# The planner that orders a mixer's engines is changed, the softmax scaling leaves the score chain, and two gates move forward

## The chip, the cores and the metric

One NeuronCore of a Trainium2 chip. The time is the device time of one execution in microseconds; a kernel's time is the median over its runs. Engines are named as in the profile: PE is TensorE (PEld its weight loads), ACT ScalarE, DVE VectorE, POOL GpSimd, SP SyncE.

## What is computed

An encoder block on 512 tokens and 16 learned meta tokens, width 1024, all in float32: a half-step SwiGLU feed-forward (hidden width 2816), a mixer, and a second half-step feed-forward. The mixer is where the change lies:

```python
u = rms_norm(h, mix_norm)
z = u @ w_in                      # 42 blocks of 128 columns
y_a = hgrn2_bidir(zq_a, zi_a, zf_f, zf_b, zg_a, lb_f, lb_b, out_norm)   # 4 heads, K = V = 128
y_b = axial_gqa(zq_b, zk_b, zv_b, q_norm, k_norm, cos, sin)             # 8 heads of 64, 2 of keys
mixed = sigmoid(zgate_a) * (y_a @ w_up_a) + sigmoid(zgate_b) * (y_b @ w_up_b)
h = h + mixed @ w_out
```

`hgrn2_bidir` is a gated linear recurrence run forward and backward over chunks of 128 tokens; `axial_gqa` is softmax attention with normalised and rotated queries and keys.

## The kernel before, in words

Activations lie transposed: 128 features on the partitions, tokens along the free axis. Each weight block (128 output columns by 1024 inputs, 512 KB) is split by ScalarE and VectorE into two fp32r parts, `whi` (a cast, L90) and `wlo` (a subtraction, L92), and so are the activations (`xh`, `xl`). A product is three matmuls for each 128 inputs: a **main triple**. A block for 512 tokens is 24 matmuls, a block for all 528 is 48 in two PSUM banks.

**Mixer, main stream.** For each of four heads the main stream computes blocks of `z`: `Z_QB` (attention queries), `Z_FB`, `Z_QA`, `Z_FF`, `Z_G`, `Z_I` (backward gate, recurrence query, forward gate, output gate, value); head 0 has `Z_KB` and `Z_VB` too. Then come seven branch-b gates (`Z_GB`, `EARLY`), and eight products with `w_up_b`, each followed by its product with the gate (L1187 on). After that everything runs in a plain order: branch a, `w_out`, the second feed-forward. `scaled` (L663) takes a block out of PSUM with VectorE.

**Side chains.** Beside it run Python generators that issue instructions step by step: `prepare` (norms and rotation of keys and queries), `scores` (L841: 32 rows of attention, each a score step of four matmuls into the one `S` tile, the row's maximum `nm` on VectorE, `nr` and the Exp on ScalarE, then the reciprocal of the sum and the scaling `pr`), `turned` (L876: five transposes of a row, `ph` and `pl`, and after four rows the product with V), `gla` (L980: each head's recurrence as seven levels; a level is ScalarE's copy `ks`, four float32 matmuls into `gs`, VectorE's products on `Z` and `tot` in `grow`, and a predicated copy into `A`) and `gla_finish` (L1069: four transposes, state products, 14 closing matmuls, an rms norm by Newton steps, four transposes).

**What sets the order.** Instructions of PE, ACT, DVE and POOL stand in the order in which the Python code issues them (manual schedule, L625 and L699), and each engine takes its own in that order. The class `Order` (L161) is a planner at build time: it keeps a model time `t` of TensorE, a time at which each other engine is free, and for every chain the model time at which its next step is ready. After each triple of the main stream `tick` (L232) lets `pump` (L225) issue every chain step that is ready at `t`. Where the main stream needs something (`need`, L235), chain steps are issued, earliest first, until it is there; `t` jumps to each step's readiness. Each engine call is charged in `account` (L174). For a matmul of a side chain:

```python
if cur is not self.main:
    self.t = max(self.t, cur.ready)              # L181
...
cur.ready, cur.eng = self.t + self.DRAIN, eng    # L188, DRAIN = 0.3
```

so each matmul of a step is taken to start no earlier than 0.3 us behind the one before it. A transpose is charged 0.11 us, an fp32r matmul n/2400 + 0.0133, a float32 one at least 4n/2400 + 0.005 (L183 to L187).

Three PSUM banks `mm` are shared by the main stream and the chains: `has_bank`, `take`, `give` (L243 to L258). `weights` (L648) hands the main stream a block's two parts, adds a small chain that makes the next block's parts (two buffers each), makes it ready 0.5 us later (L657) and issues steps until its cast has been issued (L659). Three buffers `tm` (L670) hold blocks of queries, keys and values; a fourth user waits for the first one's release.

Of the kernel before, what the change touches and what calls it, by code (L numbers as in the profile page):

```python
# [15 lines left out]
P = 128  # L16
# [144 lines left out]
class Order:  # L161
# [12 lines left out]
    def account(self, eng, op, args, kw):  # L174
        out = kw.get("out", args[0])
        n, cur = 1, self.cur
        for d in out.shape[1:]:
            n *= d
        if eng == "pe":
            if cur is not self.main:  # L180
                self.t = max(self.t, cur.ready)  # L181
            if op == "transpose":
                self.t += 0.11  # L183
            elif args[1].dtype == F32R:
                self.t += n / 2400 + 0.0133
            else:
                self.t += max(4 * n / 2400, 0.06) + 0.005  # L187
            cur.ready, cur.eng = self.t + self.DRAIN, eng  # L188
            return
        if eng == "act":  # L190
            d = n * 0.000916 + 0.115
            if "accum_out" in kw:
                d += 0.19
            f = args[2] if len(args) > 2 else kw.get("func")
            if f in (AF.Exp, AF.Sigmoid, AF.Sqrt) and f != self.table:
                self.table = f
                d += 1.28
        elif op == "reciprocal":
            d = 0.0065 * n + 0.12
        elif op == "tensor_reduce":  # L200
            d = 0.70
        elif op == "memset":
            d = 0.15
        else:
            d = (n + 160) / 960
        start = max(self.free.get(eng, 0.0), cur.ready + (self.HOP if cur.eng != eng else 0.0))
        self.free[eng] = cur.ready = start + d
        cur.eng = eng
# [4 lines left out]
    def ready(self, ch):  # L213
        return ch.ready if ch.wait is None or ch.wait() else float("inf")
# [28 lines left out]
    def has_bank(self):  # L243
        return bool(self.banks)

    def take(self):

        if self.cur is self.main:
            self.need(self.has_bank)
        r = min(self.banks)  # L250
        self.banks.remove(r)
        if self.cur is self.main:
            self.t = max(self.t, r)
        else:
            self.cur.ready = max(self.cur.ready, r)
# [24 lines left out]
def block_kernel(tc, xT, wg1, wu1, wd1, w_in, wup, wout, wg2, wu2, wd2, params,  # L280
# [18 lines left out]
    with (tc.tile_pool(name="persist", bufs=1) as sp, tc.tile_pool(name="wts", bufs=1) as wp,  # L299
# [271 lines left out]
        with tc.tile_pool(name="f1", bufs=1) as ft:  # L571
# [40 lines left out]
            order = [Z_QB, Z_KB, Z_FB, Z_VB, Z_QA, Z_FF, Z_G, Z_I]  # L612
            for hd in range(1, HEADS):
                order += [c + hd for c in (Z_QB, Z_FB, Z_QA, Z_FF, Z_G, Z_I)]
            plan = [w_in[c] for c in order]
            tiles = [w_in[Z_GB + c] for c in range(KT)] + [wup[c][:, 512:] for c in range(KT)]
            plan += tiles[:EARLY] + tiles[KT:KT + 5] + tiles[EARLY:KT] + tiles[KT + 5:]
# [7 lines left out]
        with tc.tile_pool(name="mix", bufs=1) as mp, tc.manual_schedule(engines={pe.engine}):  # L625
# [22 lines left out]
            def weights():  # L648
# [5 lines left out]
                if not W.ready:  # L654
# [4 lines left out]
                    il.need(lambda: not W.ahead_raw)  # L659
# [38 lines left out]
            with (tc.tile_pool(name="heads", bufs=1) as hp, tc.tile_pool(name="small", bufs=1) as mn,  # L698
# [139 lines left out]
                waiting = []  # L838
                out_of = [0]

                def scores():  # L841

                    for j in range(HEADS):
# [3 lines left out]
                        for e in range(2):  # L847
                            for c in range(4):
# [17 lines left out]
                                yield  # L866
                                dve.reciprocal(sm, sm)
                                yield
                                act.activation(pr, pr, AF.Copy, scale=sm)
                                waiting.append((j, e, c, pr, il.cur.ready))  # L870
# [5 lines left out]
                def turned():  # L876

                    for j in range(HEADS):
                        yb.append(mp.tile([P, SEQ], F32, name="yb", tag="yb", bufs=4))
                        for e in range(2):  # L880
# [3 lines left out]
                            for c in range(4):  # L884
                                yield lambda: waiting
                                _, _, _, pr, ready = waiting.pop(0)
# [18 lines left out]
                            yield lambda: il.banks and out_of[0] < 3  # L905
# [46 lines left out]
                def gla_inputs(hd):  # L952
# [6 lines left out]
                    yield  # L959
                    if hd:  # L960
# [3 lines left out]
                    yield  # L964
                    scaled(Z[:, 0], zcols(T))
# [23 lines left out]
                def gla_head(hd, Z, tot, q, v):  # L989
# [3 lines left out]
                    ks = kbuf()  # L993
                    dve.tensor_tensor(ks, Z[:, 0, :SEQ], Z[:, 3, :SEQ], ALU.add)
                    first = il.cur.ready
# [143 lines left out]

                for gen in (prepare(), scores(), turned(), gla(), gla_finish()):  # L1140
                    il.add(gen)
                queries(0)
                gi = gla_inputs(0)
                kz, ksq = tmp("keys"), tmp("keys")
# [8 lines left out]
                for hd in range(1, HEADS):  # L1153
                    if hd > 1:
                        il.need(lambda: f"att{hd - 2}" in il.done)
# [3 lines left out]

                def gate(sg):  # L1160
                    (o, _), = zcols(SEQ)
                    dve.tensor_tensor(sg, o, R[:, :SEQ], ALU.mult)
                    give()
# [7 lines left out]
                sgs = []  # L1171
                for c in range(EARLY):
                    sg = mp.tile([P, SEQ], F32, name="mixb", tag="mb", bufs=4) if c < 4 else tmp(f"b{c}")[:, :SEQ]
                    gate(sg)
                    sgs.append(sg)
# [3 lines left out]
                ybl = hp.tile([P, 4, SEQ], F32R, name="ybl", tag="pl")  # L1179
                for j, y in enumerate(yb):  # L1180
                    split((ybh[:, j, :], ybl[:, j, :]), y, slice(0, SEQ))
                    YB.append((ybh[:, j, :], ybl[:, j, :]))
                for sg in sgs:
                    act.activation(sg, sg, AF.Sigmoid)

                mixb = []
                for c in range(KT):  # L1187
                    if c == 5:
                        sgs.append(tmp()[:, :SEQ])
                        gate(sgs[-1])  # L1190
                        act.activation(sgs[-1], sgs[-1], AF.Sigmoid)
                    b = branch(YB)
                    m = sgs[c] if c < 4 else mp.tile([P, SEQ], F32, name="mixb", tag="yb", bufs=4)
# [115 lines left out]
```

## Time and profile before

| | us |
|---|---|
| median of 3 runs | 1239.66 (1239.02 to 1242.03) |
| the profiled execution | 1241.96 |
| its span, first to last instruction | 1240.1 |
| mean granted TensorE clock | 0.988 of full |

The mixer's interleaved part, with side chains beside the main stream, runs from about 383 to 756 us of the span; before it lies the first feed-forward, behind it branch a, `w_out` and the second. Busy shares are of a stretch's length; a row of TensorE tells its start and, in brackets, how long it had been idle and which instruction's end released it. Matmuls overlap in the records, so spacing is read from start to start.

### The profile page before, as it was taken

The numbers are of one execution on the slowest core, as the hardware profiler recorded it, in microseconds if no ns is written. First come the engines' busy times: TensorE is split into PE (matmuls) and PEld (weight loads), VectorE is DVE, ScalarE is ACT, GpSimd is POOL, SyncE is SP. The second block draws the span as 40 slices with busy tenths as digits, with TensorE's granted clock in tenths as the row PEclk, the third lists the DMA queues.
The fourth block names the chain that finished last, engine by engine and source line by source line (L and its number), as shares of the span: only waits on it lengthen the run. The fifth ranks groups of instructions, "written<-read, shape, count | busy, mean of one in ns | idle before, by whom it ended". The sixth has DMA issues, their size and how long they took to land. (4 is left out here: it accounts for less than half of the span.)

```text
span 1240.1 us, 19340 instructions
## 1 busy us (share of the span) xinstructions
PE 1185.0 (96%) x7765; PEld 1077.0 (87%) x7765; DVE 870.3 (70%) x1409; ACT 577.1 (47%) x979; POOL 100.0 (8%) x77
## 2 busy tenths in 40 slices
PE   8999999999999987898888999999999999999998
PEld 8999999999998965786776887888888998998997
DVE  7988658748757786477686765545598875875863
ACT  5545435425554555545736424333454543543541
POOL 1011000001021000000000000112200201101100
PEclk8999999999999998899999999999999999999999
DMA  6233333322132210021020112323422423323213
GB/s 225 61 109 120 91 97 107 99 86 103 45 97 99 86 35 17 18 68 52 18 69 18 52 60 70 109 88 117 136 85 86 136 86 102 119 86 102 103 52 119
DMA packets 34233, 106.21 MB, mean 86 GB/s; under 512 B 3936, under 2 KB 4320, under 8 KB 34144
## 3 DMA queue, kind: packets, MB, share of 16 engines
q1 hardware_dynamic: 33984, 104.44, 26.1%
q8 instruction: 61, 1.00, 0.3%
q0 software_dynamic: 160, 0.54, 0.1%
q14 instruction: 28, 0.23, 0.1%
HBM read 102.87 MB, written 2.10 MB: 85 GB/s over the span
## 5 line engine op out<-in xcount | busy, mean ns | idle before, releaser
L101 ACT CAST whi<-raw 128x1024 fp32r<-128x1024 f32 (+2 forms) x179 | 150.0, 839 | 251.7 <-PE mm L294 88.6
L102 DVE TENSOR_TENSOR wlo<-raw,whi 128x1024 fp32r<-128x1024 f32 (+2 forms) x179 | 177.6, 995 | 20.6 <-ACT whi L101 18.6
L276 PE MATMUL mm<-xh,whi 128*128 128x512 f32 (+1 forms) x352 | 115.5, 365 | 0.0
L276 PE MATMUL mm<-xl,whi 128*128 128x512 f32 (+1 forms) x352 | 109.2, 348 | 0.0
L276 PE MATMUL mm<-xh,wlo 128*128 128x512 f32 (+1 forms) x352 | 109.0, 347 | 0.0
L102 DVE TENSOR_TENSOR wlo<-sums,whi 128x1024 fp32r<-128x1024 f32 x72 | 87.5, 1217 | 25.0 <-ACT whi L101 24.8
L101 ACT CAST whi<-sums 128x1024 fp32r<-128x1024 f32 x72 | 75.4, 1050 | 62.4 <-DVE sums L128 20.9
L133 POOL TENSOR_TENSOR sums<-raw 128x512 f32<-128x512 f32 x36 | 58.8, 1634 | 492.6 <-DVE wlo L102 483.4
L276 PEld LDWEIGHTS mm<-xh,wlo 128*128 128x128 f32 x352 | 62.3, 192 | 8.2
L276 PEld LDWEIGHTS mm<-xh,whi 128*128 128x128 f32 x352 | 62.9, 193 | 7.3 <-issue 0.7
L276 PEld LDWEIGHTS mm<-xl,whi 128*128 128x128 f32 x352 | 62.7, 193 | 5.4
L294 PE MATMUL mm<-hh,wlo 128*128 128x256 f32 (+1 forms) x218 | 63.0, 334 | 0.0
L294 PE MATMUL mm<-hh,whi 128*128 128x256 f32 (+1 forms) x218 | 62.8, 333 | 0.1
L294 PE MATMUL mm<-hl,whi 128*128 128x256 f32 (+1 forms) x218 | 62.9, 332 | 0.0
L471 PE MATMUL mm<-xl,whi 128*128 128x264 f32 (+1 forms) x216 | 61.3, 284 | 0.0
L471 PE MATMUL mm<-xh,whi 128*128 128x264 f32 (+1 forms) x216 | 61.2, 283 | 0.0
L471 PE MATMUL mm<-xh,wlo 128*128 128x264 f32 (+1 forms) x216 | 61.1, 283 | 0.0
L276 ACT CAST whi<-raw 128x1024 fp32r<-128x1024 f32 (+1 forms) x41 | 39.4, 965 | 36.9 <-PE mm L276 27.8
L294 PE MATMUL mm<-xh,whi 128*128 128x512 f32 (+2 forms) x152 | 51.4, 365 | 2.7 <-ACT xh L375 2.7
L276 DVE TENSOR_TENSOR wlo<-raw,whi 128x1024 fp32r<-128x1024 f32 (+1 forms) x41 | 45.8, 1116 | 9.8 <-ACT whi L276 9.6
L294 PE MATMUL mm<-xl,whi 128*128 128x512 f32 (+2 forms) x152 | 51.8, 367 | 0.0
L294 PE MATMUL mm<-xh,wlo 128*128 128x512 f32 (+2 forms) x152 | 51.2, 363 | 0.0
(351 smaller groups left out, 3574.3 us busy)
## 6 DMA issues: line engine op xcount, KB each, us to landing
raw<-in_wg SPq DMA_DIRECT2D x43, 512.0 KB, 3.9
raw<-in_wu SPq DMA_DIRECT2D x43, 512.0 KB, 3.3
raw<-in_w_in SPq DMA_DIRECT2D x42, 512.0 KB, 3.3
raw<-in_wd SPq DMA_DIRECT2D x48, 384.0 KB, 3.1
raw<-in_wd SPq DMA_DIRECT2D x16, 256.0 KB, 2.7
raw<-in_wup SPq DMA_DIRECT2D x16, 256.0 KB, 2.7
raw<-in_wout SPq DMA_DIRECT2D x8, 512.0 KB, 3.3
h<-in_xT SPq DMA_DIRECT2D x4, 528.0 KB, 6.7
```

The lines of the kernel that those rows point to most:

```text
L101: nc.scalar.copy(hi[:, c], src)
L102: nc.vector.tensor_tensor(lo[:, c], src, hi[:, c].bitcast(F32), ALU.subtract)
L133: nc.gpsimd.tensor_tensor(t[:, E], r0[:, E], r1[:, E], ALU.add)
L276: return f(*args, **kw)
L294: pe.matmul(o, a[:, sl], b[:, cols], start=(k == 0 and i == 0), stop=(k == n - 1 and i == 2))
L471: pe.matmul(o, a[:, sl], b[:, kk, :], start=(start and kk == 0 and i == 0), stop=(kk == 3 and i == 2), skip_group_check=True)
```

## The change

Nothing is computed otherwise. In the planner: the drain is charged once for a run of matmuls in one step; ScalarE's accumulation costs 0.2 us, a per-partition scale 0.17 more, wide `tensor_scalar` runs at (n + 160)/1400 ns; a chain that waits for a bank becomes ready when the bank is free by the model, and the main stream, where it must wait for a bank, lets chains step until then. `weights` issues the cast of the next block at once. In `scores` the reciprocal and the scaling become a chain of their own, `scaled_rows`, and `turned` takes the rows by number. `Z_FF` goes ahead of `Z_QA` and of the wait for `began`. The gates `Z_GB` 0 and 1 go ahead of the blocks of heads 2 and 3, in the order of the loads as well. The keys' squares use a buffer of `pr` instead of a `tm`. Sigmoids of the gates follow each branch product instead of standing ahead of all. The first sum of a recurrence head no longer delays its transposes in the model, and the splits of the four `yb` are charged from one start.

```diff
@@ -177,7 +177,7 @@
         if eng == "pe":
-            if cur is not self.main:
+            if cur is not self.main and cur.eng != eng:
                 self.t = max(self.t, cur.ready)
@@ -190,7 +190,9 @@
             if "accum_out" in kw:
-                d += 0.19
+                d += 0.2
+            if not isinstance(kw.get("scale", 1.0), (int, float)):
+                d += 0.17
             f = args[2] if len(args) > 2 else kw.get("func")
@@ -201,6 +203,8 @@
             d = 0.15
+        elif op == "tensor_scalar" and n > 64:
+            d = (n + 160) / 1400
         else:
@@ -211,7 +215,8 @@
     def ready(self, ch):
-        return ch.ready if ch.wait is None or ch.wait() else float("inf")
+        w = True if ch.wait is None else ch.wait()
+        return max(ch.ready, 0.0 if w is True else w) if w else float("inf")
@@ -241,12 +246,20 @@
     def has_bank(self):
-        return bool(self.banks)
+        return self.banks and min(self.banks) + 1e-6
...
         if self.cur is self.main:
-            self.need(self.has_bank)
+            while not self.banks or min(self.banks) > self.t:
+                ch = min(self.chains, key=self.ready, default=None)
+                r = self.ready(ch) if ch else float("inf")
+                if self.banks and min(self.banks) <= r:
+                    break
+                assert r < float("inf"), "nothing can go on"
+                self.t = max(self.t, r)
+                self.step(ch)
         r = min(self.banks)
@@ -609,12 +622,13 @@
-            order = [Z_QB, Z_KB, Z_FB, Z_VB, Z_QA, Z_FF, Z_G, Z_I]
+            order = [Z_QB, Z_KB, Z_FB, Z_VB, Z_FF, Z_QA, Z_G, Z_I]
             for hd in range(1, HEADS):
-                order += [c + hd for c in (Z_QB, Z_FB, Z_QA, Z_FF, Z_G, Z_I)]
+                order += [Z_GB + hd - 2] if hd > 1 else []
+                order += [c + hd for c in (Z_QB, Z_FB, Z_FF, Z_QA, Z_G, Z_I)]
             plan = [w_in[c] for c in order]
             tiles = [w_in[Z_GB + c] for c in range(KT)] + [wup[c][:, 512:] for c in range(KT)]
-            plan += tiles[:EARLY] + tiles[KT:KT + 5] + tiles[EARLY:KT] + tiles[KT + 5:]
+            plan += tiles[HEADS - 2:EARLY] + tiles[KT:KT + 5] + tiles[EARLY:KT] + tiles[KT + 5:]
             for c in range(KT):
@@ -656,7 +670,7 @@
                     il.add(W.parts(act, dve))
-                    il.need(lambda: not W.ahead_raw)
+                    il.step(il.chains[-1])
                     W.fetch()
@@ -835,8 +849,15 @@
-                waiting = []
+                pending = []
                 out_of = [0]
+                def scaled_rows(i, pr, sm):
+                    yield
+                    dve.reciprocal(sm, sm)
+                    yield
+                    act.activation(pr, pr, AF.Copy, scale=sm)
+                    pending[i] = pr, il.cur.ready
@@ -863,11 +884,8 @@
                                 act.activation(pr, s[:, WIDE], AF.Exp, bias=nr, scale=r, accum_out=sm)
-                                yield
-                                dve.reciprocal(sm, sm)
-                                yield
-                                act.activation(pr, pr, AF.Copy, scale=sm)
-                                waiting.append((j, e, c, pr, il.cur.ready))
+                                il.add(scaled_rows(len(pending), pr, sm))
+                                pending.append(None)
                         il.done.add(f"att{j}")
@@ -882,8 +900,9 @@
                             for c in range(4):
-                                yield lambda: waiting
-                                _, _, _, pr, ready = waiting.pop(0)
+                                i = (2 * j + e) * 4 + c
+                                yield lambda: len(pending) > i and pending[i] is not None
+                                pr, ready = pending[i]
                                 il.cur.ready = max(il.cur.ready, ready)
@@ -902,7 +921,7 @@
                                 yield
-                            yield lambda: il.banks and out_of[0] < 3
+                            yield lambda: out_of[0] < 3 and il.has_bank()
                             av, v = mm(), VS[j // 2]
@@ -957,12 +976,12 @@
                     yield
+                    scaled(Z[:, 0], zcols(T))
+                    yield
                     if hd:
...
                     scaled(zi[:, 0], zcols(SEQ))
-                    yield
-                    scaled(Z[:, 0], zcols(T))
                     yield
@@ -991,8 +1010,10 @@
                     ks = kbuf()
+                    ready = il.cur.ready
                     dve.tensor_tensor(ks, Z[:, 0, :SEQ], Z[:, 3, :SEQ], ALU.add)
-                    first = il.cur.ready
+                    first, il.cur.ready = il.cur.ready, ready
+                    yield
                     o = four()
@@ -1137,11 +1158,24 @@
+                def gate(sg):
+                    (o, _), = zcols(SEQ)
+                    dve.tensor_tensor(sg, o, R[:, :SEQ], ALU.mult)
+                    give()
+                sgs = []
+                def early(c):
+                    sg = mp.tile([P, SEQ], F32, name="mixb", tag="mb", bufs=4) if c < 4 else tmp(f"b{c}")[:, :SEQ]
+                    gate(sg)
+                    sgs.append(sg)
...
                 gi = gla_inputs(0)
-                kz, ksq = tmp("keys"), tmp("keys")
+                kz, ksq = tmp("keys"), hp.tile([P, TP], F32, name="ksq", tag="pr", bufs=3)[:, :T]
                 scaled(kz, zcols(T))
@@ -1152,15 +1186,11 @@
                     if hd > 1:
+                        early(hd - 2)
                         il.need(lambda: f"att{hd - 2}" in il.done)
...
-                def gate(sg):
-                    (o, _), = zcols(SEQ)
-                    dve.tensor_tensor(sg, o, R[:, :SEQ], ALU.mult)
-                    give()
@@ -1168,28 +1198,25 @@
-                sgs = []
-                for c in range(EARLY):
-                    sg = mp.tile([P, SEQ], F32, name="mixb", tag="mb", bufs=4) if c < 4 else tmp(f"b{c}")[:, :SEQ]
-                    gate(sg)
-                    sgs.append(sg)
+                for c in range(HEADS - 2, EARLY):
+                    early(c)
                 il.need(lambda: "attention" in il.done)
...
                 ybl = hp.tile([P, 4, SEQ], F32R, name="ybl", tag="pl")
+                ready = il.t
                 for j, y in enumerate(yb):
+                    il.main.ready = ready
                     split((ybh[:, j, :], ybl[:, j, :]), y, slice(0, SEQ))
                     YB.append((ybh[:, j, :], ybl[:, j, :]))
-                for sg in sgs:
-                    act.activation(sg, sg, AF.Sigmoid)
...
                         gate(sgs[-1])
-                        act.activation(sgs[-1], sgs[-1], AF.Sigmoid)
                     b = branch(YB)
+                    act.activation(sgs[c], sgs[c], AF.Sigmoid)
                     m = sgs[c] if c < 4 else mp.tile([P, SEQ], F32, name="mixb", tag="yb", bufs=4)
```

## Rows read from the trace of the kernel before

**Rows 1.** The page, busy us (share of the span) and instructions of each engine.

```profile
PE 1185.0 (96%) x7765; PEld 1077.0 (87%) x7765; DVE 870.3 (70%) x1409; ACT 577.1 (47%) x979; POOL 100.0 (8%) x77
```

**Rows 2.** Busy time by stretch of the mixer: from:to and length in us, then busy us (and instructions) of PE, PEld, DVE, ACT, POOL, then the granted TensorE clock, the DMA engines' busy share and GB/s.

```profile
432.00:530.00 98.00, 77.45 (x434) 63.57 (x433) 64.19 (x130) 56.00 (x119) 0.00 (x0) 0.91 0.08 26
530.00:575.00 45.00, 41.73 (x255) 36.09 (x254) 35.52 (x65) 17.08 (x23) 0.18 (x2) 1.00 0.21 71
575.00:607.00 32.00, 24.93 (x163) 20.29 (x162) 19.48 (x47) 20.97 (x54) 0.00 (x0) 1.00 0.05 17
607.00:655.00 48.00, 43.82 (x275) 38.05 (x274) 39.92 (x74) 23.30 (x34) 0.44 (x2) 1.00 0.17 56
655.00:692.00 37.00, 30.04 (x197) 25.59 (x196) 21.91 (x53) 25.22 (x58) 0.42 (x1) 0.95 0.08 29
692.00:745.00 53.00, 52.84 (x288) 44.23 (x286) 35.26 (x52) 16.30 (x31) 0.00 (x0) 1.00 0.17 55
...
432.00:692.00 260.00, 217.96 (x1315) 183.59 (x1314) 181.02 (x365) 142.57 (x286) 1.04 (x5) 0.96 0.12 39
```

**Rows 3.** Waits of TensorE in 432 to 756 us: who waited <- for whom: us in total, times, longest us.

```profile
PE gs L276 <- DVE A L276: 17.1, 15, 3.7
PE at L276 <- DVE pl L276: 6.6, 6, 1.8
PE mm L276 <- ACT on L276: 4.0, 2, 2.0
...
PE mm L276 <- DVE ybl L276: 1.1, 1, 1.1
```

**Rows 4.** Timeline of TensorE, 575 to 607 us: start us, us, engine, line, operation, out<-in, shapes, count [idle before <- what ended it]. An `S` row is half of a score step, an `at` row a turn of probabilities, `gs` a level, `mm<-xh` the first third of a main triple.

```profile
575.79 1.16 PE L276 MATMUL gs<-Z,ks 128*128 128x128 f32 x8 [0.20 <-ACT ks L276]
576.70 0.48 PE L276 MATMUL mm<-xh,whi 128*128 128x512 f32 x1
...
581.01 0.48 PE L276 MATMUL mm<-xh,whi 128*128 128x512 f32 x1
...
583.76 0.48 PE L276 MATMUL mm<-xh,whi 128*128 128x512 f32 x1
...
591.24 0.61 PE L276 MATMUL mm<-vt,A 128*128 128x128 f32 x4
...
594.29 0.49 PE L276 MATMUL S<-kh,qst 128*128 128x256 f32 x2
...
599.32 0.66 PE L276 MATMUL mm<-ident,on 128*128 128x128 f32 x4 [2.02 <-ACT on L276]
...
600.51 0.60 PE L276 MATMUL at<-ident,pr 128*128 128x128 f32 x4
...
600.98 0.49 PE L276 MATMUL S<-kh,qst 128*128 128x256 f32 x2
...
601.55 0.39 PE L276 MATMUL mm<-xh,whi 128*128 128x512 f32 x1
601.78 0.40 PE L276 MATMUL mm<-xl,whi 128*128 128x512 f32 x1
```

**Rows 5.** Timeline of VectorE, same columns: the scaling of head 2's `Z_FF` block and of its `Z_G` block.

```profile
575.61 0.74 DVE L276 TENSOR_TENSOR Z<-mm,R 128x256 f32<-128x256 f32 x2
...
607.02 0.68 DVE L276 TENSOR_TENSOR zi<-mm,R 128x512 f32<-128x512 f32 x1
```

**Rows 6.** Busy time in the five stretches at half clock, columns as in rows 2: the first of them, and the sum and mean of all five.

```profile
444.87:448.28 3.41, 3.41 (x15) 3.04 (x14) 3.15 (x4) 2.00 (x4) 0.00 (x0) 0.50 0.00 0
...
sum 20.49, PE 20.17 PEld 17.57 DVE 11.86 ACT 10.08 POOL 0.00; mean PE 4.03 PEld 3.51 DVE 2.37 ACT 2.02 POOL 0.00
```

**Rows 7.** Timeline of TensorE, columns as in rows 4: a level ahead of the first of these five.

```profile
443.43 1.58 PE L276 MATMUL gs<-Z,ks 128*128 128x128 f32 x8 [2.24 <-ACT ks L276]
```

**Rows 8.** Groups of instructions in 432 to 756 us, shapes apart: line, engine, operation, out<-in, shapes, count | busy us, mean ns of one | idle us before them <- what ended it.

```profile
L276 DVE TENSOR_TENSOR wlo<-raw,whi 128x1024 fp32r<-128x1024 f32 x24 | 29.3, 1221 | 6.3 <-ACT whi L276 6.2
L276 ACT CAST whi<-raw 128x1024 fp32r<-128x1024 f32 x24 | 25.1, 1047 | 9.2 <-PE mm L276 5.7 <-issue 3.4
L276 ACT ACTIVATE pr<-S,nr,yq 128x528 f32<-128x528 f32 x31 | 24.5, 792 | 1.0
L276 ACT ACTIVATE pr<-pr,sm 128x528 f32<-128x528 f32 x32 | 23.6, 736 | 3.8 <-DVE sm L276 3.8
...
L276 DVE TENSOR_REDUCE nm<-S 128x1 f32<-128x528 f32 x31 | 21.6, 698 | 1.0 <-PE S L276 0.7
...
L276 DVE TENSOR_TENSOR Z<-Z,tot 128x1056 f32<-128x1056 f32 x16 | 20.0, 1252 | 3.5 <-PE gs L276 3.5
...
L276 ACT ACT_TABLE_LOAD x5 | 6.4, 1283 | 0.1
...
L276 DVE RECIPROCAL sm<-sm 128x1 f32<-128x1 f32 x32 | 5.1, 160 | 25.7 <-ACT pr L276 25.7
```

**Rows 9.** The page, DMA issues: out<-in, queue, kind, count, KB each, median us from issue to landing.

```profile
raw<-in_w_in SPq DMA_DIRECT2D x42, 512.0 KB, 3.3
```

**Rows 10.** Timeline of ScalarE, columns as in rows 4: sigmoids of the first four gates ahead of the branches.

```profile
747.19 2.21 ACT L276 ACTIVATE mixb<-mixb 128x512 f32<-128x512 f32 x4
```

**Rows 11.** Waits of ScalarE in 432 to 756 us, columns as in rows 3.

```profile
ACT whi L276 <- PE mm L276: 5.7, 3, 2.6
```

## The prediction, made before the change was run

> **What bounds the kernel now.** I read the page's engine shares first, then busy time by stretch, then what TensorE waits for, then its timeline. TensorE is busy 96% of the span and VectorE 70% [rows 1], so only a place where TensorE idles can give anything. The change touches the mixer alone, and the mixer's interleaved part from 432 to 692 us holds 260 - 218.0 = 42.0 us of TensorE idle time [rows 2]. It is uneven: 20.6 us of 98 in 432 to 530, 7.1 of 32 in 575 to 607 and 7.0 of 37 in 655 to 692 (21, 22 and 19%), but 3.3 of 45, 4.2 of 48, and 0.2 of 53 in the two stretches between and the one behind. The dense stretches are not lighter in side work for VectorE: it is busy 79 and 83% of 530 to 575 and 607 to 655, and only 61 and 59% of the two poor ones at 575 and 655. So no engine is full where TensorE idles. TensorE takes its instructions in the written order, and the next one waits for a product of VectorE or ScalarE: 17.1 us for the copy of a level's scores (`A`), 6.6 for `pl`, then two waits of 2 us for `on` [rows 3].
>
> The timeline of 575 to 607 us tells why the order is so [rows 4]. Between the group of 575.79 and the wait of 599.32 come only four triples of the main stream's matmuls (three each; 576.70, 581.01, and two from 583.76), everything else is side chains. The block that owns these triples, head 2's `Z_G` block, begins behind the scaling at 575.61 and is scaled at 607.02 [rows 5]: 31 us for 24 matmuls which, at the 0.23 us from 601.55 to 601.78 [rows 4], need 5.5 us.
>
> **The cause, in the planner's own terms.** L181 and L188 add the drain of 0.3 us between every two matmuls that one chain issues in a row. A score step of four matmuls is charged 4 x 0.12 + 3 x 0.3 = 1.39 us; the trace has 0.57 (600.98 to 601.55) [rows 4]. The turn of one row, five transposes, is charged 0.55 + 1.2 = 1.75 us; the trace has 0.47 (600.51 to 600.98). A level, four float32 matmuls, 1.77 us against 0.91 (575.79 to 576.70). The 14 matmuls that close a head 6.95 against 3.05 (591.24 to 594.29). Between 575.8 and 599.7 there are 5 score steps, 4 turns, one product with V (8 x 0.3 over), 2 levels and the end of a head (4-, 5-, 14- and 4-operation steps, 6.9 over): 4.5 + 4.8 + 2.4 + 1.8 + 6.9 = 20.4 us that the planner believes TensorE worked and it did not, in 24 us. So it takes ScalarE and VectorE for done when they are not, finds another chain step ready, and lets the main stream starve.
>
> **The change, part by part.** No instruction is added or removed; all is order, and one buffer.
> - The drain once per step (L180). It removes the 20.4 us of false time, so the main stream's triples come between the chain steps. Is there main work enough? From 575.9 to gla head 1's end at 601 the stream may issue `Z_G`, `Z_I`, the moved gate and the next `Z_QB` before it meets a wait for that head: about 4 x 5.5 = 22 us beside 24.9 us of busy TensorE [rows 2] of which only some 5 us is main. Yes. In 655 to 692 five gates follow freely. In 432 to 530 `Z_FF` now stands ahead of the wait for `began0`, and a gate ahead of `att0`. Nearest rows for the result: the stretches where the same chains ran with a fed stream, idle 7.3, 8.7 and 0.3% [rows 2]. I take 8%, the two with the fuller VectorE: 167 us of poor stretches become some 145 with 12 us idle, instead of 34.6. Gain 22 us; bounds 0 (the waits remain) and 42.2.
> - The clock. Five stretches of together 20.5 us run at half clock (granted 0.50, the 1.2 GHz level), TensorE busy in 20.2 of them [rows 6]; at 2.4 GHz that work needs 10.1 us less. The first comes 1.4 us behind the end of a 2.24 us wait at 443.43 [rows 7]; the wait of 2.02 us that ends at 599.32 [rows 4] drew none. Gain between 0 and 10.1; I take half, 5 us, since shorter waits remain. The Trainium skill, page "TensorE: Matmul & The Clock Gate", Part 1, says that half clock is the default and activity lifts it; by that rule all five go with their waits and the sum would be 5 us more. The trace agrees for the first of the five and not for the wait at 599.32.
> - Scores no longer behind the scaling. The step's chain loses a reciprocal of 0.16 and a scaling of 0.74 us [rows 8]. Two score steps in a row lie 6.7 us apart in the poor stretch (594.29 and 600.98) [rows 4], and what remains of their chain, 0.57 on TensorE, 0.70 and 0.79 [rows 8], is a third of that with its short steps and handovers. Attention ends long before the branches need it, so on the path this is worth 0 by itself; it only makes rows ready sooner. At most it is inside the 22 us.
> - Two gates and `Z_FF` moved. Each gate brings its load (512 KB, 3.3 us to landing [rows 9], on SP's queue in the same order as the blocks), its cast on ScalarE (1.05 us), its split (1.22) and a scaling on VectorE [rows 8]. A block takes TensorE 5.5 us or more, so the load is hidden by two raw buffers; if it were late, 3.3 us once. Cost 0; it is the filler of the first point. POOL's queue is passed by nothing.
> - Banks by time, the finer ScalarE and VectorE costs, the keys' squares in a `pr` buffer: they sharpen the order; the squares are read before the first row's probabilities. 0, bounds -2 and +2 (one of the single waits of [rows 3] goes or comes).
> - Sigmoids behind their branch. Seven stood in one batch ahead of a head's `on` and the branch weights, the first four at 2.2 us [rows 10]; the largest wait of the branches there is 1.1 us [rows 3]. Each now lies under 12 matmuls of its branch (12 x 0.23 = 2.8 us). Table loads: 1.28 us each, five in this part [rows 8], all between Exp and Sigmoid; no Exp is left at the branches, so none is added. Gain 0 to 1.1, I take 0.
> - The weight cast placed at once (L659). The cast of the next block goes into ScalarE's order where the block begins, ahead of steps ready within the next 0.5 us; it must wait until TensorE has left the block before. ScalarE's casts sat idle 9.2 us in all before 24 casts, 5.7 of it on TensorE [rows 8]. Behind a waiting cast stand `nr`, the Exp, `ph` and `ks`, and TensorE's turns and levels wait for them. Bounds: -6 (the 5.7 us go) and +9 (the idle that the casts show comes twice). I take 0, hidden by the main stream, which runs beside.
>
> **Sum:** -22 - 5 = -27 us. The profiled execution took 1241.96 us (span 1240.1, 1.9 around it): 1215. It lies 2.3 us over the median of the runs, 1239.66, so the forecast is **1213 us**.
>
> **Rivals.**
> - *VectorE crowds.* It is busy 181.0 of 260 us in 432 to 692 [rows 2], 70%; squeezed to 234 us that is 77%, about what the dense stretches bear at 8% idle. If the squeezed stretches queue as the one at 432 does (its rate stays), only 575 and 655 improve, 14.0 to 5.5 us idle, and no clock returns but one stretch's 1.7: about -10 us, 1230. For it: the chain of a level is VectorE's with its product of 1.25 us (`Z`) [rows 8]. Against: 61 and 59% in the poor ones.
> - *Everything goes.* Idle near 0.3% throughout and full clock: 34.6 - 2 + 10.1 = 43 us, 1197. For it: 692 to 745 runs nine level steps without idling. Against: there no attention row runs.
> - *Slower: the cast blocks ScalarE.* Place: L656 to L659, at each of the 27 block starts (24 full casts and 3 of half size). The longest wait of a cast for TensorE is 2.6 us [rows 11]. If all 27 wait so, ScalarE stands 70 us, against 9 now. TensorE's share in it decides: the gain of 27 is gone when over 27/61, some 45%, of it reaches TensorE; at 60% the kernel takes 1240 + 10 = 1250. For it: the same page of the Trainium skill, in its section on the array of 32x32, calls ScalarE's queue strict first-in first-out, so everything behind a waiting cast waits. Against: ScalarE is busy only 55% of 432 to 692 [rows 2] and the fed stream itself needs no ScalarE for 5.5 us at a time.
> - *Nothing changes.* Chain steps may be late by real latency, not by the planner; the waits move to other instructions: 1240.
>
> **How the numbers follow.** A measurement here can tell about 0.3%, 3.7 us, from no change. Forecast 0.68, VectorE crowds 0.13, everything goes 0.05: faster 0.86. Nothing changes 0.05. The blocking cast 0.09. The range runs from the case in which all goes, 1197, to a crowding with half of its gain, 1235; left out are slower, no change and the last of the low end, under 0.2.
>
> **What would show it.** Right: the three poor stretches vanish; between two score steps stand one to four main triples; `Z_G` of head 2 takes under 20 us; total TensorE wait of the mixer's part 15 to 25 us, `gs <- A` below 8; at most three half-clock stretches; VectorE near 77%. Wrong: TensorE waits over 35 us in all (the planner was not the cause); ScalarE's casts idle over 25 us on TensorE (the cast blocks); long waits of TensorE at 690 to 740, with no matmul of the main stream, because the last head's levels come too late.

## The result, and the profile after

The changed kernel takes **1191.1 us** (1190.3 to 1192.7, 4 runs) against 1239.5: ratio 0.961, interval 0.959 to 0.962, 48 us less. It was forecast faster, at 1213 with a range of 1197 to 1235; the direction held and the size did not: the time lies 6 us under the range. The profiled execution took 1190.4 us, its span 1188.6. The kernel before was run again beside each experiment, at 1239.5 to 1241.7 us, so below kernels are compared by their ratios to it.

The page's engine shares, which answer to [rows 1]; DVE and ACT work about as long as before (within 6 us), TensorE's busy time is 18.3 us shorter though its 7765 matmuls are the same:

```profile
PE 1166.7 (98%) x7765; PEld 1068.4 (90%) x7765; DVE 865.0 (73%) x1409; ACT 578.5 (49%) x981; POOL 98.6 (8%) x77
```

Busy time by stretch after, columns as in [rows 2]; the first row is the whole interleaved stage, from the start of the first scaled block of the mixer (`tm<-mm,R`) to the start of the last gated branch-b product (`mixb<-mm,tm`), and the last row is the part of the attention rows and levels:

```profile
386.20:726.70 340.50, 329.52 (x2004) 286.60 (x2004) 263.50 (x514) 195.87 (x376) 0.71 (x7) 0.99 0.16 56
432.00:530.00 98.00, 95.14 (x619) 84.41 (x618) 82.86 (x168) 60.98 (x118) 0.22 (x2) 1.00 0.16 55
530.00:575.00 45.00, 44.62 (x283) 38.44 (x282) 36.48 (x76) 31.82 (x67) 0.22 (x2) 1.00 0.14 48
575.00:607.00 32.00, 30.59 (x190) 26.99 (x190) 29.89 (x59) 16.77 (x32) 0.00 (x0) 0.96 0.17 61
607.00:655.00 48.00, 47.60 (x297) 41.87 (x296) 34.39 (x71) 31.89 (x66) 0.11 (x1) 0.99 0.15 49
655.00:686.00 31.00, 30.76 (x181) 25.87 (x180) 25.93 (x45) 17.70 (x35) 0.00 (x0) 1.00 0.08 26
432.00:686.00 254.00, 248.71 (x1564) 217.58 (x1562) 209.55 (x415) 159.16 (x314) 0.56 (x5) 0.99 0.14 50
```

The same stage in the kernel before:

```profile
387.10:778.60 391.50, 346.05 (x2008) 292.97 (x2009) 267.95 (x513) 194.02 (x374) 1.19 (x7) 0.97 0.15 48
```

The stage lost 391.5 - 340.5 = 51.0 us, all that the two profiled spans differ by (51.5) but 0.5. The split into poor and dense stretches is gone: even the two at 530 and 607, idle 7 and 9% before, idle 0.8%. What TensorE still waits for in 432 to 727 us, columns as in [rows 3]:

```profile
PE mm L289 <- DVE wlo L289: 2.1, 2, 1.3
PE gs L289 <- ACT ks L289: 1.4, 1, 1.4
PE mm L289 <- ACT ybh L289: 1.0, 1, 1.0
PE mm L289 <- ACT on L289: 1.0, 2, 0.6
...
PE gs L289 <- DVE A L289: 0.5, 1, 0.5
```

Of the 17.1 us for `A` 0.5 are left, and the turns' 6.6 for `pl` are gone. The timeline of TensorE, columns as in [rows 4], shows how the order looks now:

```profile
575.51 1.49 PE L289 MATMUL gs<-Z,ks 128*128 128x128 f32 x8
576.69 0.54 PE L289 MATMUL mm<-xh,whi 128*128 128x512 f32 x1
577.07 0.40 PE L289 MATMUL mm<-xl,whi 128*128 128x512 f32 x1
577.30 0.39 PE L289 MATMUL mm<-xh,wlo 128*128 128x512 f32 x1
577.53 0.39 PE L289 MATMUL mm<-xh,whi 128*128 128x512 f32 x1
...
578.22 0.60 PE L289 MATMUL at<-ident,pr 128*128 128x128 f32 x4
578.65 0.27 PE L289 MATMUL am<-ident,pr 128*16 128x128 f32 x1
578.68 0.49 PE L289 MATMUL S<-kh,qst 128*128 128x256 f32 x2
...
579.25 0.40 PE L289 MATMUL mm<-xh,whi 128*128 128x512 f32 x1
579.50 0.40 PE L289 MATMUL mm<-xl,whi 128*128 128x512 f32 x1
...
580.64 1.13 PE L289 MATMUL gs<-Z,ks 128*128 128x128 f32 x8
...
604.03 1.52 PE L289 MATMUL gs<-Z,ks 128*128 128x128 f32 x8 [1.41 <-ACT ks L289]
```

Between the level of 575.51 and that of 580.64 stand four main triples, a turn and a score step, and nothing waits. `Z_G` is not strung out any more; the scalings that answer to [rows 5], `Z_FF`, `Z_QA` and `Z_G` of head 2, in the timeline of VectorE:

```profile
602.53 0.77 DVE L289 TENSOR_TENSOR Z<-mm,R 128x256 f32<-128x256 f32 x2 [0.52 <-PE mm L289]
...
617.11 0.68 DVE L289 TENSOR_TENSOR zi<-mm,R 128x512 f32<-128x512 f32 x1
...
622.88 0.69 DVE L289 TENSOR_TENSOR zi<-mm,R 128x512 f32<-128x512 f32 x1 [1.29 <-PE mm L289]
```

`Z_G` takes 5.8 us (617.11 to 622.88) where it took 31. `Z_QA` in front of it, which now stands behind the wait for `began`, takes 14.6, with the wait of 1.41 us at 604.03 and a stretch at half clock in it.

**Where the 51 us came from.** From start to start, TensorE's time in the stage falls into idle time (from the recorded end of a matmul to the next start), time in stretches at half clock, and the rest. Half of the time at half clock is put down to the clock. Before: 44.0 idle, 22.7 at half clock. After: 9.5 idle, 6.7 at half clock. So 34.5 us are idle time, 8.0 the clock, and 8.5 are neither: the same matmuls at full clock took 334.8 us before and 326.3 after. (The stage begins and ends with VectorE, so in each run the parts add up to some 1.3 us less than its length.)

Most of the third part stands beside the waits, where the records don't show it as idle time. Two rows of the kernel before:

```profile
578.41 0.27 PE L276 MATMUL am<-ident,pr 128*16 128x128 f32 x1
580.13 1.13 PE L276 MATMUL gs<-Z 128*128 128x128 f32 x8 [1.45 <-DVE A L276]
```

The transpose is recorded as 0.27 us and the idle time counts from its end, so the two starts lie 1.72 us apart for a wait of 1.45. After, the same transpose at 578.65 is followed 0.03 us later by a score step: its 0.27 us cost nothing when the next one is ready. The Trainium skill, "Perfetto Trace Analysis", section on the per-engine timelines, says that the end of a TensorE record is an estimate. The rows agree: a recorded end can lie behind the start of the next matmul.

Over the whole stage the effect is smaller than in this pair of rows. Waits over 0.15 us fell from 47 to 15. Held against the mean spacing of its kind and shape in e7, e10 and e12, where little waits, the matmul in front of such a wait took 0.16 us more before (7.6 us in all) and 0.18 after (2.7), and the first one behind it 0.07 and 0.08 (3.1 and 1.2 us). That is 5.0 + 1.9 = 6.9 of the 8.5 us; what the other 1.6 are, no run shows. Over the runs below, the time at full clock is longest where waits are many, but it does not go in step with them: with 13 to 16 waits it lies anywhere from 324.4 to 327.8.

| run | stage us | idle us | waits | at half clock us | rest at full clock us |
|---|---|---|---|---|---|
| before | 391.5 | 44.0 | 47 | 22.7 | 334.8 |
| e4 | 400.1 | 43.2 | 51 | 40.0 | 335.5 |
| e2 | 382.1 | 35.9 | 42 | 23.8 | 333.0 |
| e3 | 353.3 | 17.1 | 26 | 6.6 | 331.8 |
| e5 | 358.8 | 20.7 | 16 | 23.7 | 325.0 |
| e11 | 347.0 | 15.2 | 16 | 9.2 | 325.9 |
| after | 340.5 | 9.5 | 15 | 6.7 | 326.3 |
| e14 | 338.8 | 8.0 | 14 | 3.5 | 327.8 |
| e6 | 346.1 | 12.8 | 13 | 15.1 | 324.4 |
| e1 | 347.1 | 10.9 | 11 | 16.3 | 326.8 |
| e7 | 331.3 | 4.7 | 7 | 0.0 | 325.4 |

### The profile page after: what moved, and what is told of

Read it like the earlier page. It is cut to its first block, busy times and chain, and to the rows that moved or that the text cites. A ratio compares the mean times of both kernels' runs of the same rounds, so it can differ in the third digit from the quotient of the medians.

```text
span 1188.6 us, 19335 instructions
## 1 busy us (share of the span) xinstructions
PE 1166.7 (98%) x7765; PEld 1068.4 (90%) x7765; DVE 865.0 (73%) x1409; ACT 578.5 (49%) x981; POOL 98.6 (8%) x77
## 3 DMA queue, kind: packets, MB, share of 16 engines
q1 hardware_dynamic: 33984, 104.44, 26.4%
## 4 chain that ended last, share of the span: by engine, by line
PE 90%; DVE 5%; ACT 2%; DMA 2%; issue 1%; SPq 0%; POOL 0%; ACTq 0%; DVEq 0%
PE mm L289 21%; PE mm L307 20%; PE mm L484 14%; PE at L484 9%; PE at L307 5%; PE am L307 4%; PE gs L484 4%; PE S L307 4%; PE gs L289 3%; PE am L484 2%; DVE wlo L102 1%; PE S L289 1%; PE at L289 1%; DMA raw<-in_wu 1%; ACT whi L101 1%
## 5 line engine op out<-in xcount | busy, mean ns | idle before, releaser
L289 ACT CAST whi<-raw 128x1024 fp32r<-128x1024 f32 (+1 forms) x41 | 39.6, 965 | 38.9 <-PE mm L289 32.5
L578 DVE SCALAR_TENSOR_TENSOR h<-mm,h 128x512 f32<-128x512 f32 (+2 forms) x40 | 20.9, 544 | 41.4 <-PE mm L307 41.3
L289 DVE TENSOR_TENSOR Z<-Z,tot 128x512 f32<-128x512 f32 (+1 forms) x48 | 40.7, 875 | 13.8 <-PE gs L289 6.8
```

The costliest lines, as they stand in the source:

```text
L289: return f(*args, **kw)
L578: dve.scalar_tensor_tensor(h[c][:, cols], o, 0.5, h[c][:, cols], ALU.mult, ALU.add)
```

## The experiments

The theory is that the planner's false TensorE time (0.3 us between the matmuls of one step) caused the waits; the rival, that the gain is a sum of many parts or hangs on the release of the scores.

**e1: the drain alone, on the kernel before.**

```diff
-            if cur is not self.main:
+            if cur is not self.main and cur.eng != eng:
```

Expected: 

> The kernel before with L181 alone changed (the drain is charged once for a run of matmuls in one step). If the planner's false TensorE time is the cause (theory drain): three quarters of the gain or more, 1203 us or less, TensorE's waits in the mixer below 20 us and at most two half-clock stretches. If the gain needs the other parts too (theory sum: banks by time, cast, scores, gates): 1215 to 1230, waits of 25 us or more. If the drain does nothing by itself: 1236 to 1243.

Measured: 1195.3 us, ratio 0.964 (0.962 to 0.965). One line of the planner gives 46 of the 48 us. Its stage, columns as in [rows 2]:

```profile
387.60:734.80 347.20, 334.88 (x2009) 291.10 (x2009) 264.01 (x514) 198.10 (x378) 0.91 (x6) 0.98 0.16 55
```

**e2: the changed kernel without it** (the same line, the other way).

Expected: 

> The changed kernel with the old charge of 0.3 us between the matmuls of a step (L180 undone), all else as changed. Theory drain: the poor stretches come back, 1225 to 1240. Theory sum: 1200 to 1215. If the drain does nothing: 1191, within 4.

Measured: 1232.9 us, 0.993 (0.992 to 0.995). All other parts together give 8 us. The waits are back, and one that the kernel before had small, the score step's (the last row is the kernel before's):

```profile
PE at L289 <- DVE pl L289: 8.8, 9, 2.6
PE S L289 <- ACT pr L289: 8.8, 11, 2.5
PE gs L289 <- DVE A L289: 7.9, 8, 2.1
...
PE S L276 <- ACT pr L276: 1.6, 4, 0.5
```

**e3: half of the charge, on the changed kernel.**

```diff
-            if cur is not self.main and cur.eng != eng:
-                self.t = max(self.t, cur.ready)
+            if cur is not self.main:
+                self.t = max(self.t, cur.ready - (0.15 if cur.eng == eng else 0.0))
```

Expected: 

> The changed kernel with half of the old charge, 0.15 us between the matmuls of a step. Theory drain, with an effect in proportion: midway between the changed kernel and e2. With a threshold (the main stream is fed as soon as the charge is below what it needs): within 6 us of 1191. Also: TensorE's own slots (start to start less idle time) and its idle time should fall together if late operands cost both; if the slots stay at the length of before while the idle time falls, the shorter slots of the changed kernel have another cause.

Measured: 1202.4 us, 0.969 (0.967 to 0.970): by the ratios 10 us of the 41 that the whole charge costs. The effect is graded but not in proportion. From e2 to here idle time falls by 18.8 of the 26.4 us that lie between e2 and the changed kernel, the time at full clock by 1.2 of 6.7 (the table). So the two do not fall together, and by the expectation's own test the shorter time at full clock has a cause beside the waits, which stays open.

**e4: the scaling in its own chain, on the kernel before** (the diff's `scaled_rows` and `pending`, nothing else).

Expected: 

> The kernel before with the scaling of a row in a chain of its own, nothing else. Theory drain: no more than 6 us from 1239.5, either way, since attention is not what the main stream waits for. If the release of the scores carries the change: 1215 or less.

Measured: 1250.2 us, 1.007 (1.006 to 1.009): slower by 9, where at most 6 were expected. The waits lie elsewhere than before (`S <- pr` 1.6 us there, `pl` 6.6 and `A` 17.1):

```profile
PE S L276 <- ACT pr L276: 15.7, 18, 1.8
PE at L276 <- DVE pl L276: 12.2, 12, 1.4
PE gs L276 <- DVE A L276: 7.7, 9, 1.6
```

But they are not longer in all: idle time is 43.2 us against 44.0. The 9 us are the clock, 40.0 us at half clock against 22.7 (half of the difference is 8.7; the table). Its stage, columns as in [rows 2]:

```profile
386.70:786.90 400.20, 355.50 (x2009) 300.24 (x2010) 268.59 (x514) 195.54 (x374) 1.19 (x7) 0.95 0.14 47
```

Why the same idle time, in other places, drew more half clock is not shown.

**e5: the changed kernel with reciprocal and scaling back in the score chain.**

```diff
-                                il.add(scaled_rows(len(pending), pr, sm))
-                                pending.append(None)
+                                yield
+                                dve.reciprocal(sm, sm)
+                                yield
+                                act.activation(pr, pr, AF.Copy, scale=sm)
+                                pending.append((pr, il.cur.ready))
```

Expected: 

> The changed kernel with the reciprocal and the scaling back in the scores chain, so that a score step waits for the row in front to be scaled. With a fed main stream the attention rows are not what TensorE waits for: 1191, within 3 us. If the release of the scores is what feeds the turns in time: 1196 or more. If it disturbs as it did alone on the kernel before (1250 against 1241): below 1187.

Measured: 1208.5 us, 0.974 (0.972 to 0.975): 16 us slower, so on the changed kernel the release of the scores carries weight. I had priced it at nothing. In the profiled stage, 18.3 us longer, 11.2 are idle time and 8.5 the clock; the time at full clock is 1.3 shorter (the table).

**e9: drain and scores, both on the kernel before.**

Expected: 

> The kernel before with two parts: the drain once per step and the scaling of a row in a chain of its own. The release of the scores cost 9 us alone on the kernel before and brought 17 on the changed one. If its worth hangs on the planner's TensorE time being true: 1183 to 1192, at or under the changed kernel. If it hangs on the other parts (banks, cast, order): 1196 or more.

Measured: 1199.3 us, 0.967 (0.963 to 0.971), not to be told from e1. So beside the drain alone the release brings nothing that shows, and without it among all other parts 16 us are lost. Its worth hangs on the rest (cast, banks, order); which of them, these runs don't tell.

**e6: the changed kernel with `Z_FF` and the gates in their old places** (the order of the loads too).

Expected: 

> The changed kernel with Z_FF behind the wait for began again and no gate moved forward (seven gates at the end). If these blocks are the filler that the chains need (the prediction's view of them): 1196 to 1206, with waits of TensorE at 440 to 530 and around 550 to 570. If there is main work enough without them: 1191, within 3 us.

Measured: 1196.3 us, 0.963 (0.961 to 0.965); its interval overlaps that of the changed kernel. 2 to 3 us by the ratios, at most 7: without these blocks the stream still has work enough for nearly all of the gain, which is the second expectation. The waits that the first one names are back in part: 9.5 us in 440 to 530, against 2.8 in the changed kernel, and none around 550 to 570.

**e8: the old rule for banks** (`has_bank` is a truth value, `take` uses `need`).

Expected: 

> The changed kernel with the old rule for PSUM banks (a chain may take a bank that is free only later in the model, and the main stream's time jumps to the bank's). If TensorE's single waits behind on, st and zg came from it: 1194 to 1200, with two or three waits of 1 to 2 us for ACT on or DVE zg back. If not: 1191, within 2 us.

Measured: 1188.1 us, 0.957 (0.955 to 0.958), 5 us faster than the changed kernel by the ratios. Neither of the two expectations: here this part costs a little. Beside the corrected charge of e13 it is worth 7 us (e15 below), so its sign hangs on the rest.

**e7: the old place of the weight cast.**

```diff
-                    il.step(il.chains[-1])
+                    il.need(lambda: not W.ahead_raw)
```

Expected: 

> The changed kernel with the cast of the next block issued by need, in the order of readiness, the model time jumping up to 0.5 us a block. If the cast placed at once held ScalarE (the prediction's slower rival): faster than 1189. If the false 0.5 us for each of 27 to 33 blocks mattered like the drain's false time (13 to 16 us of model time against some 150): 1193 to 1197. If neither: 1191, within 2 us.

Measured: 1184.7 us, 0.954 (0.952 to 0.955): faster, by 9 us when the ratios are compared. Of the three expectations this is the one of a ScalarE held by the cast. But ScalarE's waits of casts for TensorE in the stage are no shorter, 34.6 us in e7 and 32.5 in the changed kernel (the waits of ScalarE, `whi <- PE mm`). The old line does two things, so two kernels each do one.

**e10: the cast at once, the model time put forward.**

```diff
                     il.step(il.chains[-1])
+                    il.t = max(il.t, il.main.ready)
```

Expected: 

> The changed kernel, the cast placed at once, but the model time of TensorE put forward by 0.5 us at each block as before. e7 undid the whole part and was 6 us faster. If the time put forward is what helps (the model's TensorE is else too early): 1183 to 1187. If the place of the cast in the order is what helps: 1189 to 1196.

Measured: 1183.1 us, 0.953 (0.951 to 0.954).

**e11: the cast in order of readiness, the model time set back.**

```diff
-                    il.step(il.chains[-1])
+                    now = il.t
+                    il.need(lambda: not W.ahead_raw)
+                    il.t = now
```

Expected: 

> The changed kernel with the cast issued in the order of readiness, behind the steps that are ready within 0.5 us, but with the model time of TensorE set back afterwards. If the place of the cast in the order helps (chain steps get in front of it on ScalarE and in front of the block on TensorE): 1183 to 1187. If the time put forward helps: 1189 to 1194.

Measured: 1198.6 us, 0.966 (0.964 to 0.967). The time put forward is what helps; the cast's old place by itself costs 6 us. So the mended planner's TensorE seems too fast: it charges a main matmul of 512 columns n/2400 + 0.0133 = 0.227 us. Over the stage the mean from start to start of the matmuls of 512 columns, outside idle time and half clock, is 0.240. Most take 0.23, and so does the first of a triple behind a score step (21 of them; 579.25 to 579.50 in the timeline after is 0.25); the first one behind a level takes 0.32 on average (18; the longest is the 0.38 from 576.69 to 577.07), behind a row's transposes 0.31 (8).

**e13: the charge corrected instead.**

```diff
-                self.t += n / 2400 + 0.0133
+                self.t += n / 2400 + 0.0267
```

Expected: 

> The changed kernel with fp32r matmuls charged n/2400 + 0.0267 us instead of + 0.0133, so 240 ns for 512 columns, as measured. If the rest is the planner's TensorE running ahead of the real one: 1181 to 1186, idle 5 us or less. If the jump at the block's start helps for another reason (it lets chain steps go in front of the block): 1189 to 1196.

Measured: 1184.4 us, 0.954 (0.952 to 0.957), idle 4.9 us: as expected.

**e14: the model time put forward twice as far** (`il.t += 1.0`).

Expected: 

> The changed kernel with the model time put forward by 1.0 us at each block, twice e10's. If the model time has a true value near e10's: slower than e10, 1186 to 1195, since chain steps are then again issued before their operands are there. If any false time at the block's start helps: 1183 or less. From the other side, the false time in the chains (e3, 0.15 us a matmul) cost 11 us.

Measured: 1190.5 us, 0.959 (0.957 to 0.961): the gain is gone again. Of the three jumps tried, 0, 0.5 and 1.0 us a block, the middle one is the fastest.

**e12: old cast and old banks. e15: corrected charge and old banks.**

Expected: 

> The changed kernel with both the old cast (e7) and the old rule for banks (e8). If their effects add (6 and 4 us): 1179 to 1183. If both only remove the same remaining waits (9.5 us of idle in all, 4.7 left in e7): 1183 to 1187. If the orders of single steps decide, without rule: anything up to 1195.

Expected: 

> The changed kernel with the charge of e13 and the old rule for banks of e8. If both remove what is left: 1178 to 1183, as e12. If single steps decide: 1183 to 1192.

Measured: e12 1180.9 us, 0.951 (0.950 to 0.953), the fastest of all, 60 us under the kernel before; it can't be told from e10. e15 1191.1 us, 0.960 (0.958 to 0.963): no sum of e13 and e8. Within some 11 us of the best (e12 to e15 by the ratios) the parts do not add up; that the order of single steps decides there is my reading, not shown. The stages of e7, e10, e12 and e13 in that order:

```profile
386.80:718.10 331.30, 325.20 (x2009) 284.31 (x2010) 263.26 (x513) 195.08 (x376) 1.02 (x7) 1.00 0.17 57
```

```profile
389.10:720.40 331.30, 326.00 (x2009) 285.39 (x2010) 263.13 (x514) 195.99 (x376) 0.99 (x7) 0.99 0.17 57
```

```profile
387.70:719.20 331.50, 326.93 (x2009) 285.70 (x2010) 263.34 (x513) 196.40 (x376) 1.02 (x7) 0.99 0.17 57
```

```profile
388.60:723.40 334.80, 328.43 (x2009) 287.56 (x2010) 262.94 (x514) 196.55 (x376) 1.02 (x7) 0.99 0.17 57
```

They hold 4.6 to 6.4 us of time without a running matmul; the matmuls themselves took 324 to 326 us at full clock in every run with ten waits or fewer.

## Why the prediction was right in its cause and wrong in its size

- **The cause** (false time of 0.3 us a matmul starves the stream) is shown: one line gives 46 us (e1), its reversal costs 41 (e2), half of it 10 (e3).
- **The idle time, -22: wrong.** The step that failed is "I take 8%", the idle share of the stretches at 530 and 607 us as what a fed stream leaves. Those stretches had the same fault. Their waits are nearly all the levels' `gs <- A`, charged 1.77 us against 0.91, and with the charge they went (idle 0.8% in both); the waits in 530 to 575 and in 607 to 655 of the kernel before, columns as in [rows 3]:

```profile
PE gs L276 <- DVE A L276: 3.2, 4, 1.5
```

```profile
PE gs L276 <- DVE A L276: 3.2, 4, 1.6
PE at L276 <- ACT pr L276: 0.7, 1, 0.7
```

Of my three nearest rows the third, 0.3% in 692 to 745, was the one without the fault's waits. Measured: -34.5.
- **The clock, -5: too small**, -8.0. The rule that activity lifts the half clock, so that all five stretches go with their waits (the Trainium skill, "TensorE: Matmul & The Clock Gate", Part 1), came nearer. The trace mostly agrees: of the time at half clock 6.7 of 22.7 us is left. One stretch is from 389.64, where the kernel before has one at 390.25, ahead of the part that I looked at; the other, left in place of the five of [rows 6], follows the wait of 1.41 us that ends at 604.03. How many waits there are does not settle it: e1, with 11, kept 16.3 us at half clock.
- **A term was missing, -8.5**: beside the idle time shown, a wait costs some 0.2 us in the matmuls on either side of it. That covers 6.9 us; 1.6 stay open. 34.5 + 8.0 + 8.5 = 51.0.
- **Main work enough: right.** e6 takes the filler away and loses 2 to 3 us, which can't be told from none.
- **Scores, 0 by itself: wrong both ways**, +9 alone (e4), -16 among the other parts (e5), nothing beside the drain alone (e9).
- **The cast at once, 0: wrong by some 9 us, not by the mechanism of the slower rival.** That one needed ScalarE held at the block's start; casts did wait longer for TensorE (13.8 us before 25 full casts in 432 to 756 us, against 5.7 in [rows 8]), yet e10 keeps the cast at once and is among the fastest. What the change lost here is the 0.5 us a block by which the old line put the model time forward: given back alone (e10) it brings the 9 us, and so does a higher charge for the matmuls (e13, 8 us).
- **Sigmoids, gain 0 and no table load added: wrong by little.** Table loads in the stage went from 8 to 10, and the last now stands ahead of a branch's cast. ScalarE's timeline, then TensorE's wait:

```profile
693.19 0.63 ACT L289 CAST whi<-raw 128x512 fp32r<-128x512 f32 x1
693.84 1.28 ACT L289 ACT_TABLE_LOAD   x1
695.13 0.63 ACT L289 ACTIVATE mixb<-mixb 128x512 f32<-128x512 f32 x1
695.67 0.60 ACT L289 CAST whi<-raw 128x512 fp32r<-128x512 f32 x1
```

```profile
697.14 0.50 PE L289 MATMUL mm<-ybh,wlo 128*128 128x512 f32 x1 [1.32 <-DVE wlo L289]
```

- **Rivals.** *VectorE crowds* falls: in 432 to 686 us it is busy 209.6 of 254, 82%, more than the 77% that I worked out, while TensorE idles 2%. *Everything goes*, priced at -43 with a chance of 0.05, is nearly what happened; my reason against it ("there no attention row runs") was no reason, since rows run in nearly every stretch now. I had seen that no engine was full and that the stream had work, and still gave the poor share of a faulty planner as the floor.
- **What would show it**: `gs <- A` under 8 us (0.5), `Z_G` under 20 (5.8) and at most three half-clock stretches (two) came; VectorE came out at 82% for the 77, and the wait of 15 to 25 us in all at 9.5.

## What to carry to other kernels

Where one engine's order is written ahead of time by a model, compare each charge of the model with start-to-start times of the trace, for every kind of step: one wrong constant was worth 4% here, and a charge 6% too low for the commonest matmul another 0.6%. Price what a repair leaves from a stretch free of the fault, not from the best stretch that still has it, and add to each wait what the records hide beside it. A part can help among others and harm or do nothing without them (the scores: -16, +9 and 0 us), so mend the model first and then try the parts one by one.

## What the runs showed of the hardware that was not expected

- A wait of TensorE cost some 0.23 us more than its idle time in the records: 0.16 in the matmul in front of it and 0.07 in the first one behind it, over the 47 waits of the kernel before.
- The same idle time in other places came with 17 us more at half clock (e4: 43.2 us idle, 40.0 at half clock; before: 44.0 and 22.7).
- A wait of 1.41 us was followed 0.65 us later by a stretch of 3.41 us at half clock, while the one of 2.02 us at 599.32 in [rows 4] drew none. The stretch of the changed kernel, columns as in [rows 2]:

```profile
604.68:608.09 3.41, 3.41 (x15) 2.94 (x14) 3.06 (x6) 0.37 (x1) 0.00 (x0) 0.50 0.43 154
```

- The first matmul of a main triple took 0.32 us behind a level and 0.31 behind a row's transposes, but 0.23, as the others of the triple, behind a score step (means in the changed kernel's stage). A planner that charges every one alike is off by 0.1 us at some steps.
